# Three operands of Vector's products moved to PSUM, and GpSimd's weight subtractions halved, in a two-block fp32 layer

## Chip, cores and metric

One Trainium2 chip, one core of it, one launch. The time is the device time of that core in microseconds (us). Before the change three runs gave 1184.07, 1188.38 and 1190.91 us, median 1188.38. Engines are called by their function here: TensorE (PE in the rows; PEld is its weight load), Vector (DVE), ScalarE (ACT), GpSimd (POOL) and SyncE (SP), which issues nearly all DMAs.

## What is computed

256 tokens of width 1024 pass two blocks, all in float32; the second also has 16 learned tokens in front, so that it works on 272 columns. Cut to what matters:

```
h    = rms_norm(x)                          # first block
proj = h @ w_in                             # 19 pieces and four gates
y_a..y_d = four mixers of proj              # gating, sparse attention, short convolution, forgetting attention
x1   = x + sum(sigmoid(gates) * (y @ w_branch)) @ w_out
x2   = rms_norm(x1)

h2   = rms_norm([meta; x2])                 # second block, mixer
proj = h2 @ w_in_2                          # f, q, k, v, z, a/b, two gates
q,k,v = silu(depthwise_conv(proj_qkv, 5))   # centred, five taps
A    = strict_lower(beta k k^T * decay)     # per head and chunk of 64 tokens
t    = (I + A)^-1                           # triangular solve
o    = gated delta rule over the chunks, in both directions
y    = gates * ((rms_norm(o) * silu(z)) @ w_delta, fft2(f) @ w_fourier)
h    = h + y @ w_out_2
out  = h + experts(rms_norm(h))             # 64 experts, two for each token
return rms_norm(out)[16:]
```

## The kernel before

**Dense products.** Activations stand feature-major: 128 features on the partitions, tokens in the columns. An fp32 product is made from two exact parts of each factor: a high part that TensorE takes as it is, and the rest. `load()` brings a weight tile in by DMA, ScalarE copies its high part (L293, `whi`), and GpSimd or Vector subtracts that from the whole (L296, `wlo`); a string of letters in `wst["lo"]` says which engine takes which tile, and in the second block's mixer it is GpSimd for most. `dense_fm` (L324) then makes three matmuls for each of eight k: high x high (L331), high x low of the activations (L332) and low of the weights x high (L336), 24 matmuls of 256 or 272 columns for one tile of 128 features, in one PSUM bank `psd`.

**PSUM.** Two kinds of tile: `bank`, one bank, four of them; and `big`, two banks, two of them. Each is given out in turn and is waited for when all are held. `big_c` gives tiles of the same shape in SBUF.

**Stages, in the order of time.** The first block's dense tiles and mixers (0 to about 371 us); the seam, where the first block's result is added up, normed and split into parts (L792 to L855), which `normed` does (L436): Vector builds two diagonal matrices with the rows' factors (L440), TensorE spreads them over the partitions into a bank `psr` (L441), Vector copies that to SBUF (L444, `rcoll`); then for eight feature tiles `x` of `xn` Vector multiplies by `rcoll` (L454), ScalarE copies the high part (L455), and Vector subtracts for the low part (L449). `normed` is called twice, in the first block from the token-major columns (`rcol`) and at the seam. At the seam the factors `rcoll` are also applied to the first two dense tiles of the second block (L847).

The mixer's dense tiles follow (k, q, v with their convolution, then the gates and z), with the delta rule's work woven between. For a convolution tile (`conv`, L996) ScalarE evicts the middle tap from the tile's bank into `acc` (L1004, a part of `ofm`), Vector adds the other four taps from the bank (L1008), ScalarE takes the tanh of the sum into another part of `ofm` (L1011), and Vector multiplies (tanh + 1) by the sum (L1012), into `kr`, `q` or `vr`. There are 24 such tiles, eight each.

For the triangular solve, blocks of 32x32 of A are gathered into `cmp` and transposed in blocks into `am` (L1378); then `substitution` makes 31 steps: step i multiplies the i x i corner of `X` by row i of `am` (L1382, result `xt`), and reduces it to the next column of `X` (L1383). 128 partitions work on 128 blocks at the same time. Its results are merged to blocks of 64 with matmuls, the scans over the chunks follow, then the output, and from some 735 us on the experts, whose weights come in 192 pieces of 1 MB.

**Order.** A scheduler places every instruction on its engine's queue by a simulated time; `weave` and `fill` in the code say how many dense matmuls go between the steps of the delta rule, and `manual_schedule` keeps the written order for some engines in some stretches (Vector's in `normed`). So a change in what an operation reads can move other instructions, too.

Of the kernel before, what the change touches and what calls it, by code (L numbers as in the profile page):

```python
# [33 lines left out]
# no DMA is issued by GpSimd: its descriptors need no room  # L34
# [23 lines left out]
# per-row parameters, broadcast to all partitions  # L58
# [24 lines left out]
def make_constants():  # L83
# [19 lines left out]
    # the transform over the positions, folded twice: cosines for the even and the odd ones, negative sines likewise  # L103
# [74 lines left out]
class Kit:  # L178
# [3 lines left out]
    def ready(self, pool, after, f=AF.Abs_reciprocal_sqrt):  # L182
        """have ACT's table for a function at hand, from the time that a value is there"""
        d = pool.tile([P, 1], F32, name="rs_ready")
        self.nc.scalar.activation(d, after, f, scale=0.0, bias=1.0)

    def rsqrt1(self, y, s, n, b):
        """y = 1/sqrt(s / n + b) from ACT's table, refined once (s: [P, cols], changed; b: [P, 1])"""
        v = self.nc.vector
        bc, bv = b  # L190
        ins = self.nc.scalar.activation(y, s, AF.Abs_reciprocal_sqrt, scale=1.0 / n, bias=bc)
        self.refine(y, s, n, bv)
        return ins
# [10 lines left out]
    def rsqrt(self, pool, y, x, tag):  # L204
        """y = 1/sqrt(x), x > 0"""
# [12 lines left out]
def body(ctx, tc, A, out, dbg=None, stage=9):  # L218
# [11 lines left out]
    # chunks of the experts' weights that come early  # L230
    fix = ctx.enter_context(tc.tile_pool(name="fix", bufs=1))

# [36 lines left out]
    def load(src, width, nsub, view=None):  # L269
        """nsub equal parts of the columns of src, each as (high, low)"""  # L270
# [8 lines left out]
        if wst["pairs"]:  # L279
            # two loads to a tile  # L280
            wst["part"] = 1024 - wst["part"]
# [3 lines left out]
        for j in range(nsub):  # L285
# [10 lines left out]
            eng.tensor_tensor(lo, rs, hi.bitcast(F32), op=ALU.subtract)  # L296
# [3 lines left out]
    def load_tiles(arr, t0, n, k, nsub=None):  # L300
        """n weight tiles of 128 columns, k rows each"""
# [3 lines left out]
    def split_act(pool, name, src, shape, scale=None, tag=None, bufs=None):  # L305
        """f32 tile -> its two exact parts"""
# [10 lines left out]
    def part(x, k, cols):  # L317
        """feature tile k, held in one or several tiles"""
# [5 lines left out]
    def dense_fm(jobs, x, c0, c1, nk):  # L324
        """jobs: (ps, (high, low), offset): ps[128 features, tokens c0:c1], all in one bank"""
# [12 lines left out]
    def dense_tm(pss, subs, x, n, nk, between=None):  # L338
        """pss[t][128 tokens, n columns]; subs cover the rows in order"""
# [17 lines left out]
    def sumsq(junk, src, n):  # L357
        """1 / root of the mean of squares over n columns of a tile, [rows, 1]"""
# [9 lines left out]
    def transpose_scaled(xT, src, rs, c0):  # L368
        """token-major src [rows, 1024], its rows times rs -> columns c0.. of the two parts of the transpose"""
# [11 lines left out]
    def delayed(tile_, src, after):  # L381
        """a load that waits for an earlier one"""
# [11 lines left out]
    # =====================================================================  # L394
    # first block
    # =====================================================================
    b2 = ExitStack()
    with ExitStack() as b1:
# [13 lines left out]
        def turn(pst, src, k, ts):  # L412
            """feature tiles k of token-major src, in PSUM"""
# [5 lines left out]
        def busy(src, n, rhs=None, ps=None):  # L419
            """the PE's clock stays up while it waits"""  # L420
# [6 lines left out]
        def gained(xn, pst, g, ks):  # L427
            """feature tiles ks times their gains"""
# [6 lines left out]
        def normed(xT, c0, xn, r, rcol, then=None, later=None):  # L435
            """columns c0.. of the two parts of the feature-major: the rows of xn times r"""  # L436
# [7 lines left out]
            V.tensor_copy(rcol, psr)  # L444
# [6 lines left out]
            with tc.manual_schedule(engines={V.engine}):  # L451
                for k in range(8):
                    x = xn[k // 4][:, k % 4]
                    V.tensor_tensor(x, x, rcol, op=ALU.mult)  # L454
                    SC.activation(xT[0][:, k, c0:c0 + S], x, AF.Copy)  # L455
                    if k:
                        low(k - 1)
# [17 lines left out]
        # its gains alone, for the token-major columns: those take the rows' factor when they leave PSUM  # L475
# [14 lines left out]
        # ---- token-major columns: c, w_idx, f, d_v, a_v  # L490
# [4 lines left out]
        for j in range(4):  # L495
# [17 lines left out]
            if j == 1:  # L513
# [4 lines left out]
                normed(hT, 0, xn, r1, bp.tile([P, S], F32, name="rcol", tag="th", bufs=3))  # L518
# [13 lines left out]
        # ---- feature-major columns  # L532
# [20 lines left out]
        def gated(o):  # L553
            """o *= silu of the next four tiles"""
# [11 lines left out]
        # ---- the meta tokens, normalised  # L566
# [9 lines left out]
        # ---- y_b: sparse latent attention  # L576
# [19 lines left out]
        def softmax_rows(lm, nk, tag):  # L596
            """lm [P, 4, nk] with its masked entries far below -> p, normalised"""
# [12 lines left out]
        def transposed_p(lm, t):  # L610
            """[P, 4, nk] -> [P (keys), key tile, 4, 128 (queries)]"""
# [50 lines left out]
        # ---- y_d: forgetting attention  # L662
# [11 lines left out]
        # columns k of R[t', h, k] = log f(t') where t' > k  # L674
# [5 lines left out]
        for t in range(2):  # L680
# [3 lines left out]
            # bank kt holds the keys of tile kt, four heads  # L684
# [28 lines left out]
        # ---- y_a: chunked spatial gating  # L713
# [22 lines left out]
        # ---- y_c: short convolution  # L736
# [17 lines left out]
        # ---- gates, branches  # L754
# [20 lines left out]
        # both norms at once, from the sums of squares of x1 and of x1 g  # L775
# [5 lines left out]
        # x1 with its gains, for the first columns of the second block: those take the rows' factor when they leave PSUM  # L781
# [54 lines left out]
        with tc.manual_schedule(engines={PE.engine, V.engine, SC.engine}):  # L836
# [5 lines left out]
            # the second norm sees x1 g over the first one's root  # L842
# [14 lines left out]
    # =====================================================================  # L857
    # second block: mixer
    # =====================================================================
    with b2:  # L860
# [5 lines left out]
        # where the chunks of the experts' weights go, in turn  # L866
# [3 lines left out]
        def buffer(i):  # L870
            """the i-th of the slots; one of 16 KB holds two"""
# [42 lines left out]
        # ---- dense tiles, in the order of their need; the other work is woven in between  # L914
# [53 lines left out]
        # convolution, silu (twice its value)  # L968
# [10 lines left out]
        def row(n, h):  # L979
            return halves(n)[h // 4][:, h % 4]  # L980
# [3 lines left out]
        def of_tile():  # L984
            """blocks of the substitution; two sums of the convolution and their tanh"""
# [4 lines left out]
        def kr_last():  # L990
            """a state of the scans; the fourier branch's input"""
# [4 lines left out]
        def conv(n, off, c0=0):  # L996
            W_ = L - c0

            def use(a, ps):
# [10 lines left out]
                th = of_tile()[:, 1024 + L * (2 + cx["n"]):1024 + L * (2 + cx["n"]) + W_]  # L1010
                SC.activation(th, acc, AF.Tanh, scale=0.5)  # L1011
                V.scalar_tensor_tensor(row(n, a)[:, c0:], th, 1.0, acc, op0=ALU.add, op1=ALU.mult)  # L1012
# [10 lines left out]
        # gate of the delta branch  # L1023
# [9 lines left out]
        # z  # L1033
# [8 lines left out]
        # fourier mixing  # L1042
# [11 lines left out]
        def fold(gs):  # L1054
            """the positions n and L - n at once, then n and L / 2 - n: sums for cosines, differences for sines, of even k and of odd k"""
# [52 lines left out]
        # ---- decays and betas  # L1108
# [6 lines left out]
        # [P, tile, (incl, rest, total), dir, head]  # L1115
        E = ex[:, :96].rearrange("p (t a d h) -> p t a d h", t=2, a=3, d=2)

        def hb(ap, hs=slice(0, 8)):
            """[P, 8] per head -> over 128 columns"""
# [78 lines left out]
        # ---- keys, token-major and feature-major  # L1198
        kn = early.tile([P, 2, 8, P], F32, name="kn")
        knT = keep([P, 8, S], "knT")  # L1200
        def l2(ss, n, tag):
            """per row factor of a doubled vector"""
# [7 lines left out]
        def meta_rows(n):  # L1210
            """the meta tokens of all heads, stacked [(head, token), 128]"""
# [52 lines left out]
        # ---- products of q and k; -beta k k^T with decay (rows: the smaller index)  # L1264
        An = keep([P, 2, 2, 8, P], "An")
        # the earlier steps of the scans, the later ones
# [41 lines left out]
        # ---- the sixteen meta tokens of all heads, stacked  # L1308
# [41 lines left out]
        # ---- (I - An)^-1: blocks of 32 by substitution, then merged  # L1350
        # (in place: forward as it stands, backward transposed)
# [13 lines left out]
        def substitution():  # L1365
# [11 lines left out]
            am = x32(big_c("am"))  # L1377
# [14 lines left out]
        def values():  # L1392
# [17 lines left out]
            # state after the meta tokens  # L1410
# [620 lines left out]
```

## Time and profile before

| | |
|---|---|
| median of three runs | 1188.38 us |
| lowest, highest | 1184.07, 1190.91 us |
| profiled execution, span from first to last instruction | 1187.4 us |
| busy in it: TensorE, Vector, ScalarE, GpSimd | 1064.7, 613.5, 437.6, 386.9 us |
| bytes moved | 307.67 MB, mean 259 GB/s |
| TensorE's granted clock, mean | 0.926 of full |

An engine's busy share is an average over stages with different limits, so the stages are looked at one by one. The profile also follows the chain of work that ended last, back from the last instruction, and gives for each idle stretch of an engine what ended it.

### The profile page before, as it was taken

Reading aid. Unit: us, or ns where it says so; the run is one execution under the profiler, and the core shown is the slowest. Engines: PE = TensorE matmul, PEld = TensorE weight load, DVE = VectorE, ACT = ScalarE, POOL = GpSimd, SP = SyncE. Lnnn points to the kernel's source line nnn. Section 1 sums busy time; section 2 is a strip of 40 time slices with the busy share of each in tenths; the row PEclk is TensorE's granted clock in tenths of the full one; section 3 lists DMA queues with packets and bytes.
Section 4 is the critical chain, followed back from the end, with each engine's and each line's share of the span. In section 5 each row is a group of like instructions: output and inputs, shape, how many; then the busy total and the mean of one; then the engine's idle time right before and its main releaser. Section 6 shows DMA issues by size and latency. Waiting matters only on the chain.

```text
span 1187.4 us, 21273 instructions
## 1 busy us (share of the span) xinstructions
PE 1064.7 (90%) x8800; PEld 855.1 (72%) x8800; DVE 613.5 (52%) x1204; ACT 437.6 (37%) x752; POOL 386.9 (33%) x232
## 2 busy tenths in 40 slices
PE   7899999999998889887999999999978778887794
PEld 7799999999998888887999998455433333333341
DVE  5977647534467998999375885232221111111112
ACT  5555535444447445543533544121111111111112
POOL 4453324456662666866645441000000000000100
PEclk9999999999998989898899999999988887788888
DMA  7444434555554333353227698999999999999993
GB/s 283 166 150 175 143 107 168 188 181 179 202 185 160 122 102 112 108 189 107 73 73 279 261 355 314 403 419 419 421 421 420 421 420 420 420 421 421 420 421 118
DMA packets 58856, 307.67 MB, mean 259 GB/s; under 512 B 5984, under 2 KB 7264, under 8 KB 33280
## 3 DMA queue, kind: packets, MB, share of 16 engines
q1 hardware_dynamic: 56528, 301.59, 65.5%
q10 hardware_dynamic: 2224, 4.65, 1.1%
q8 instruction: 71, 1.16, 0.4%
q14 instruction: 33, 0.27, 0.1%
HBM read 304.12 MB, written 2.10 MB: 258 GB/s over the span
## 4 chain that ended last, share of the span: by engine, by line
PE 59%; DMA 18%; DVE 16%; ACT 3%; issue 1%; POOL 1%; ACTq 0%; SPq 0%; DVEq 0%
DMA wexp<-in_wex_dram 17%; PE psd L331 10%; PE psd L332 10%; PE psd L336 10%; PE psgu L1780 5%; PE psg L1766 4%; PE psy L1819 4%; DVE ofm L1008 3%; DVE xt L1382 2%; PE acc L1833 2%; PE psd L350 1%; PE psd L355 1%; PE psd L349 1%; DVE X L1383 1%; DVE An L1289 1%
## 5 line engine op out<-in xcount | busy, mean ns | idle before, releaser
L296 POOL TENSOR_TENSOR wlo<-wraw,whi 128x1024 fp32r<-128x1024 f32 x115 | 283.7, 2470 | 258.5 <-ACT whi L293 134.6
L331 PE MATMUL psd<-hTh,whi 128*128 128x256 f32 (+2 forms) x1096 | 282.0, 294 | 13.6 <-DVE sz L1037 6.2
L332 PE MATMUL psd<-hTl,whi 128*128 128x256 f32 (+2 forms) x1096 | 280.2, 293 | 4.8 <-DVE hTl L449 4.8
L293 ACT ACTIVATE whi<-wraw 128x1024 fp32r<-128x1024 f32 (+1 forms) x183 | 193.0, 1064 | 172.0 <-PE psd L332 73.5
L331 PEld LDWEIGHTS psd<-hTh,whi 128*128 128x128 f32 x1096 | 215.6, 197 | 16.1 <-issue 10.6
L332 PEld LDWEIGHTS psd<-hTl,whi 128*128 128x128 f32 x1096 | 215.4, 197 | 6.5 <-DVE hTl L449 5.4
L1780 PE MATMUL psgu<-wexp,xg 128*32 128x512 f32 x1024 | 148.8, 671 | 38.0 <-DMA wexp<-in_wex_dram 37.9
L296 DVE TENSOR_TENSOR wlo<-wraw,whi 128x1024 fp32r<-128x1024 f32 (+1 forms) x68 | 121.4, 1791 | 77.0 <-PE psd L336 59.4
L336 PE MATMUL psd<-hTh,wlo 128*128 128x256 f32 (+2 forms) x1096 | 155.8, 290 | 0.0
L336 PEld LDWEIGHTS psd<-hTh,wlo 128*128 128x128 f32 x1096 | 143.0, 195 | 1.6 <-issue 1.4
L1968 POOL TENSOR_SCALAR wexp<-cst,gcol 128x128 f32<-128x128 f32 x8 | 4.7, 599 | 390.5 <-PE psgu L1780 390.5
L1780 PEld LDWEIGHTS psgu<-wexp,xg 128*32 128x32 f32 x1024 | 25.1, 113 | 116.2 <-DMA wexp<-in_wex_dram 85.7
L1766 PEld LDWEIGHTS psg<-pm,x 128*128 128x128 f32 x512 | 76.5, 231 | 16.9 <-issue 12.4
L1819 PE MATMUL psy<-wexp,at 128*32 128x256 f32 x1024 | 78.1, 413 | 9.8 <-DVE at L1809 9.2
L1766 PE MATMUL psg<-pm,x 128*128 128x128 f32 x512 | 84.4, 321 | 0.0
L1828 DVE SCALAR_TENSOR_TENSOR yl<-psy,ww,yh 128x256 fp32r<-128x256 f32 x64 | 31.0, 484 | 102.1 <-ACT yh L1827 97.0
L1786 DVE SCALAR_TENSOR_TENSOR act<-act,psgu 128x256 f32<-128x256 f32 x16 | 6.7, 421 | 136.4 <-ACT act L1785 136.4
L1827 ACT ACTIVATE yh<-psy,ww 128x256 fp32r<-128x256 f32 x64 | 30.3, 474 | 125.8 <-PE psy L1819 120.0
L1785 ACT ACTIVATE act<-psgu 128x256 f32<-128x256 f32 x16 | 6.1, 384 | 140.2 <-PE psgu L1780 140.2
L1819 PEld LDWEIGHTS psy<-wexp,at 128*32 128x32 f32 x1024 | 29.3, 113 | 37.2 <-DVE at L1809 13.5
L1768 DVE TENSOR_SCALAR xg<-psg,gcol 128x128 f32<-128x128 f32 x64 | 22.4, 351 | 62.4 <-ACT xg L1767 61.6
L1767 ACT ACTIVATE xg<-psg,gcol 128x128 f32<-128x128 f32 x64 | 23.5, 368 | 71.7 <-PE psg L1766 71.7
(644 smaller groups left out, 1688.8 us busy)
## 6 DMA issues: line engine op xcount, KB each, us to landing
wexp<-in_wex_dram SPq DMA_DIRECT2D x191, 1024.0 KB, 19.8
wraw<-in_wf_dram SPq DMA_DIRECT2D x39, 1024.0 KB, 4.9
wraw<-in_wf_dram SPq DMA_DIRECT2D x53, 512.0 KB, 4.3
wraw<-in_wbr_dram SPq DMA_DIRECT2D x8, 1024.0 KB, 5.0
wraw<-in_wtok_dram SPq DMA_DIRECT2D x4, 1160.0 KB, 6.7
wraw<-in_wout_dram SPq DMA_DIRECT2D x4, 1024.0 KB, 4.7
wraw<-in_wde_dram SPq DMA_DIRECT2D x8, 512.0 KB, 6.2
wraw<-in_wo_dram SPq DMA_DIRECT2D x8, 512.0 KB, 7.2
```

The lines of the kernel that those rows point to most:

```text
L293: SC.activation(hi, rs, AF.Copy)
L296: eng.tensor_tensor(lo, rs, hi.bitcast(F32), op=ALU.subtract)
L331: PE.matmul(ps, wh[:, ks], part(xh, k, slice(c0, c1)), start=j + k == 0, stop=False, **g)
L332: PE.matmul(ps, wh[:, ks], part(xl, k, slice(c0, c1)), start=False, stop=False, **g)
L336: PE.matmul(ps, wl[:, ks], part(xh, k, slice(c0, c1)), start=False, stop=k == nk - 1, **g)
L1008: V.scalar_tensor_tensor(acc[:, lo:hi], ps[:, lo + d:hi + d], cw(j), acc[:, lo:hi], op0=ALU.mult, op1=ALU.add)
L1382: V.tensor_tensor(tmp[:, :i, :i], X[:, :i, :i], am[:, i:i + 1, :i].to_broadcast([P, i, i]), op=ALU.mult)
L1766: PE.matmul(ps[:, f], hn[:, t, fs], self.pm[:, t].rearrange("p e c -> p (e c)"), start=t == 0, stop=t == 1)
L1780: PE.matmul(gu[32 * q:32 * q + 32, :], self.xg[:, k, 32 * q:32 * q + 32], ws[k][:, 512 * q:512 * q + 512], start=k == 0, stop=k == 7)
L1819: PE.matmul(self.ps[32 * q:32 * q + 32, cs], self.at[:, k, 32 * q:32 * q + 32], self.ws[8 + c][:, o:o + 256], start=k == 0, stop=k == 1)
L1827: SC.activation(yh, self.ps[:, cs], AF.Copy, scale=self.ww)
L1828: V.scalar_tensor_tensor(yl, self.ps[:, cs], self.ww, yh.bitcast(F32), op0=ALU.mult, op1=ALU.subtract)
```

## The change

Four edits. In `normed` Vector's eight products read the factors in PSUM (`psr`) where they lie; the copy to SBUF is ScalarE's, after the third feature tile, and is made only at the seam, where `rcoll` is needed later. In the convolution the tanh is written back into the tile's own bank `ps`, over the raw values, and the last product reads it there. `am` of the substitution lies in a `big` PSUM tile. And where GpSimd subtracts for a low part, it does so in two instructions of half the columns each (512 of 1024); Vector's subtractions stay whole. Comments are gone as well, so line numbers differ by 1 to 3.

```
@@ load
-            eng.tensor_tensor(lo, rs, hi.bitcast(F32), op=ALU.subtract)
+            for h in (slice(0, sw // 2), slice(sw // 2, sw)) if eng is G else (slice(0, sw),):
+                eng.tensor_tensor(lo[:, h], rs[:, h], hi[:, h].bitcast(F32), op=ALU.subtract)
@@ normed
-            V.tensor_copy(rcol, psr)
...
-                    V.tensor_tensor(x, x, rcol, op=ALU.mult)
+                    V.tensor_tensor(x, x, psr, op=ALU.mult)
                     SC.activation(xT[0][:, k, c0:c0 + S], x, AF.Copy)
+                    if k == 2 and rcol is not None:
+                        SC.activation(rcol, psr, AF.Copy)
...
-                normed(hT, 0, xn, r1, bp.tile([P, S], F32, name="rcol", tag="th", bufs=3))
+                normed(hT, 0, xn, r1, None)
@@ conv.use
-                th = of_tile()[:, 1024 + L * (2 + cx["n"]):1024 + L * (2 + cx["n"]) + W_]
-                SC.activation(th, acc, AF.Tanh, scale=0.5)
-                V.scalar_tensor_tensor(row(n, a)[:, c0:], th, 1.0, acc, op0=ALU.add, op1=ALU.mult)
+                SC.activation(ps, acc, AF.Tanh, scale=0.5)
+                V.scalar_tensor_tensor(row(n, a)[:, c0:], ps, 1.0, acc, op0=ALU.add, op1=ALU.mult)
@@ substitution
-            am = x32(big_c("am"))
+            am = x32(big("am"))
```

Vector's queue at the seam before, from the split of the last columns (L795) over the copy of the factors to the feature tiles of `normed`:

```order
L440 TENSOR_SCALAR diag<-cst,r__4227 128x128 x2
L795 TENSOR_TENSOR urows_3881<-xnl,uc_x 128x256 x2
L444 COPY rcoll<-psr 128x256
L454 TENSOR_TENSOR xnh<-xnh,rcoll 128x256 x2
L449 TENSOR_TENSOR hTl_3877<-xnh,hTh_3876 128x256
L454 TENSOR_TENSOR xnh<-xnh,rcoll 128x256
```

And after:

```order
L442 TENSOR_SCALAR diag<-cst,r__4278 128x128 x2
L798 TENSOR_TENSOR urows_3926<-xnl,uc_x 128x256 x2
L455 TENSOR_TENSOR xnh<-xnh,psr 128x256 x2
L450 TENSOR_TENSOR hTl_3922<-xnh,hTh_3921 128x256
L455 TENSOR_TENSOR xnh<-xnh,psr 128x256
```

The copy is gone from Vector's queue, and the products read `psr`; the order of the rest is the same. ScalarE's copy `rcoll<-psr` stands in ScalarE's queue between its third and its fourth feature tile.

Vector's queue over the last steps of the substitution before (`sz` is the product of a z tile, `Xr` the transposed result of the substitution):

```order
L1382 TENSOR_TENSOR xt<-X,am 128x26x26
L1383 TENSOR_REDUCE X<-xt 128x26
L1037 SCALAR_TENSOR_TENSOR sz<-th_5904,psd 128x256
L1037 SCALAR_TENSOR_TENSOR sz<-th_5977,psd 128x256
L1382 TENSOR_TENSOR xt<-X,am 128x27x27
...
L1382 TENSOR_TENSOR xt<-X,am 128x29x29
L1037 SCALAR_TENSOR_TENSOR sz<-th_6028,psd 128x256
L1383 TENSOR_REDUCE X<-xt 128x29
L1382 TENSOR_TENSOR xt<-X,am 128x30x30
L1037 SCALAR_TENSOR_TENSOR sz<-th_6076,psd 128x256
...
L1037 SCALAR_TENSOR_TENSOR sz<-th_6121,psd 128x256
L1387 STREAM_TRANSPOSE Xr<-X 128x1024
```

And after:

```order
L1385 TENSOR_TENSOR xt<-X,am 128x29x29
L1039 SCALAR_TENSOR_TENSOR sz<-th_5987,psd 128x256
L1386 TENSOR_REDUCE X<-xt 128x29
L1385 TENSOR_TENSOR xt<-X,am 128x30x30
L1039 SCALAR_TENSOR_TENSOR sz<-th_6061,psd 128x256
L1386 TENSOR_REDUCE X<-xt 128x30
L1385 TENSOR_TENSOR xt<-X,am 128x31x31
L1386 TENSOR_REDUCE X<-xt 128x31
L1039 SCALAR_TENSOR_TENSOR sz<-th_6113,psd 128x256
L1390 STREAM_TRANSPOSE Xr<-X 128x1024
```

Before, five of the eight z products stood ahead of the transpose `Xr`, the first two behind step 26; after, three do, the first within step 29. On TensorE's queue two dense tiles fewer stand ahead of the first merge.

## Rows read from the trace of the kernel before

**Rows 1.** Table by stages: stretch, length, busy (instructions) per engine, granted clock, DMA.

```profile
core 0: us, PE busy (x) PEld busy (x) DVE busy (x) ACT busy (x) POOL busy (x), PEclk, DMA share, GB/s
60.00:371.00 311.00, 310.51 (x2546) 303.32 (x2545) 180.49 (x222) 155.20 (x225) 144.63 (x71) 0.99 0.49 168
371.00:394.00 23.00, 15.40 (x94) 14.46 (x92) 19.59 (x43) 12.37 (x30) 10.03 (x4) 0.80 0.39 138
394.00:430.00 36.00, 33.35 (x266) 32.28 (x265) 33.57 (x71) 22.84 (x41) 24.89 (x14) 0.97 0.31 105
430.00:561.00 131.00, 114.94 (x806) 108.63 (x807) 123.41 (x237) 58.98 (x88) 87.41 (x48) 0.89 0.36 127
735.00:1140.00 405.00, 339.19 (x2774) 169.11 (x2773) 88.39 (x292) 62.91 (x153) 4.66 (x8) 0.87 1.00 414
```

**Rows 2.** Chain that ended last, 371 to 394 us: start, length, what.

```profile
372.66 4.76 DVE xt L804 x2
...
385.47 2.52 DVE xnh L454
387.99 2.49 DVE hTl L449
```

**Rows 3.** The same chain, 515 to 535 us: shares of the stretch by line.

```profile
by line: DVE xt L1382 83.5%; DVE X L1383 26.7%; issue 2.5%; DVE XRm L1344 1.9%; DVE Zm L1337 1.0%; DVE XCm L1343 1.0%
```

**Rows 4.** Timeline of Vector in the substitution: start, length, line, operation, tiles.

```profile
513.64 2.30 DVE L1382 TENSOR_TENSOR xt<-X,am 128x121 f32<-128x121 f32 x1
...
516.29 0.31 DVE L1382 TENSOR_TENSOR xt<-X,am 128x144 f32<-128x144 f32 x1
516.63 0.30 DVE L1383 TENSOR_REDUCE X<-xt 128x12 f32<-128x144 f32 x1
```

**Rows 5.** Timeline of GpSimd at the seam and in the substitution.

```profile
385.06 5.12 POOL L296 TENSOR_TENSOR wlo<-wraw,whi 128x1024 fp32r<-128x1024 f32 x2 [7.93 <-ACT hTh L455]
...
513.39 2.40 POOL L296 TENSOR_TENSOR wlo<-wraw,whi 128x1024 fp32r<-128x1024 f32 x1
```

**Rows 6.** Operations on the convolution's tile: count, ns minimum/median/maximum, first and last start.

```profile
L1008 DVE SCALAR_TENSOR_TENSOR ofm<-psd,prm,ofm x96: 454/488/501, 394.7 to 509.2; 128x270 f32<-128x270 f32 x32, 128x271 f32<-128x271 f32 x32, 128x256 f32<-128x256 f32 x16, 128x257 f32<-128x257 f32 x16
...
L1012 DVE SCALAR_TENSOR_TENSOR kr<-ofm x8: 423/442/2644, 398.2 to 420.8; 128x272 f32<-128x272 f32 x8
```

**Rows 7.** Vector's groups, 371 to 561 us: count, busy, mean ns, idle before.

```profile
L1382 DVE TENSOR_TENSOR xt<-X,am 128x1 f32<-128x1 f32 (+30 forms) x31 | 34.6, 1116 | 0.8
L1383 DVE TENSOR_REDUCE X<-xt 128x1 f32<-128x1 f32 (+30 forms) x31 | 15.5, 501 | 0.7
L1012 DVE SCALAR_TENSOR_TENSOR q<-ofm 128x258 f32<-128x258 f32 x8 | 8.7, 1083 | 0.9 <-ACT ofm L1011 0.9
...
L1012 DVE SCALAR_TENSOR_TENSOR kr<-ofm 128x272 f32<-128x272 f32 x8 | 8.0, 1025 | 1.0 <-ACT ofm L1011 1.0
L1012 DVE SCALAR_TENSOR_TENSOR vr<-ofm 128x272 f32<-128x272 f32 x8 | 6.3, 793 | 0.6 <-ACT ofm L1011 0.6
...
L1171 DVE TENSOR_TENSOR gu<-mcol 128x1 f32<-128x1 f32 x1 | 1.8, 1843 | 0.0
L1313 DVE TENSOR_SCALAR gUm<-cst,gg 128x128 f32<-128x128 f32 x1 | 1.8, 1753 | 0.0
...
L454 DVE TENSOR_TENSOR xnl<-xnl,rcoll 128x256 f32<-128x256 f32 x4 | 1.6, 412 | 0.0
```

**Rows 8.** Vector's groups of 512 columns over the whole span, by shape.

```profile
L559 DVE SCALAR_TENSOR_TENSOR ob<-th,ob 128x512 f32<-128x512 f32 x2 | 1.4, 693 | 0.1
...
L734 DVE TENSOR_TENSOR a_u<-a_u,pst 128x512 f32<-128x512 f32 x2 | 1.4, 690 | 9.9 <-PE pst L732 9.9
```

**Rows 9.** GpSimd's groups over the whole span, by shape.

```profile
L296 POOL TENSOR_TENSOR wlo<-wraw,whi 128x1024 fp32r<-128x1024 f32 x115 | 283.7, 2470 | 258.5 <-ACT whi L293 134.6 <-PE psd L336 83.2 <-PE psd L355 16.6
...
L727 POOL TENSOR_TENSOR av<-av,rows 128x512 f32<-128x512 f32 x2 | 2.6, 1310 | 1.6 <-DVE lrs L214 1.3 <-DVE av L726 0.4
```

**Rows 10.** TensorE's waits, 371 to 561 us: total us, times, longest.

```profile
PE psd L331 <- DVE sz L1037: 6.2, 1, 6.2
...
PE psd L331 <- DVE ofm L1008: 2.7, 1, 2.7
```

## The prediction

> **What bounds the kernel now.** I read the table of stages first [rows 1]. From 60 to 371 us TensorE is busy 310.51 of 311 us, so nothing that Vector or GpSimd does there can shorten it. From 735 to 1140 us the DMA share is 1.00 at 414 GB/s: the experts' weights stream in. The stream itself cannot be made shorter from this side, but it starts when the stages before it free buffers, so what is gained before 735 us should come off the end about one for one. In between lie stages where Vector is the busy engine: 371 to 394, 19.59 of 23 us; 394 to 430, 33.57 of 36; 430 to 561, 123.41 of 131. From 394 to 561 this is 157.0 of 167 us, while TensorE has 148.3 us and stands idle for 18.7. [...]
>
> Then the chain that ended last. At the seam between the blocks it runs through Vector's products and differences of 128x256, which take 2.4 to 2.5 us each [rows 2]; late in the substitution 83.5% of it is the product L1382 [rows 3].
>
> Last, why these are slow. The product of step 11, 121 elements, took 2.30 us from 513.64; that of step 12, 144 elements, 0.31 us [rows 4]. GpSimd's subtraction of a weight tile ran from 513.39 for 2.40 us [rows 5] and ended at 515.79, 0.15 us ahead of the end of the slow product. GpSimd's pair at 385.06 covers the two slow operations of the seam in the same way. So a Vector operation that starts under a GpSimd subtraction of 1024 columns may wait for its end. But not every one: the convolution's sums L1008, with one operand in PSUM and one in SBUF, took 454 to 501 ns in all of 96 cases, in the same stretches, while the products behind them, L1012, with both operands in SBUF, took up to 2644 ns [rows 6]. What waits is above all Vector with two tensors from SBUF. The change puts one of the two into PSUM in three places, and halves GpSimd's subtractions.
>
> **The change part by part.**
> *Normalisation at the seam.* On the chain stand a pair L804 (4.76 us), one L454 (2.52) and one L449 (2.49) [rows 2]. L454 reads PSUM now and should cost its undisturbed 0.41, that of the four `xnl` ones [rows 7]: -2.1. L449 and L804 keep two SBUF operands; they meet subtractions half as long, so I take half of each: -1.2 and -2.4. The DVE copy goes, a ScalarE copy of the same 256 columns comes, and Vector's fourth product waits for it. I bound that exchange by -0.4 (the copy that goes, if the new one hides under Vector's eight products) and +0.4 (if the whole of the new one is waited for), and take zero, since both are as long. Sum **-5.7**. TensorE is idle for 7.6 us there (23 - 15.40), which is room enough.
>
> *The convolution's last product.* 24 products L1012 take 8.7 + 8.0 + 6.3 = 23.0 us [rows 7]. With one operand in PSUM I take 0.43, between the least (423 ns) and the median (442) of those for `kr` [rows 6]: 24 x 0.43 = 10.3, so **-12.7**. ScalarE's tanh now writes PSUM. No row prices that; between nothing and the whole of an undisturbed product again, 0.4 for each of 24, I take nothing, since ScalarE is busy 81.8 of 167 us and hides it.
>
> *The substitution.* 31 products L1382 take 34.6 us; the reductions L1383 behind them, one SBUF tensor of the same elements, take 15.5 [rows 7], and where neither is caught they are equal: 0.31 and 0.30 at step 12 [rows 4]. **-19.1**. The one transpose that writes `am` into PSUM I count at zero: single, against 62 operations behind it.
>
> *Does reading PSUM cost more?* A product of 512 columns with an operand in PSUM (L734) takes 690 ns, one with both in SBUF (L559) 693 [rows 8]: no. [...]
>
> *Halves.* A subtraction of 1024 columns takes 2.47 at the mean, a GpSimd operation of 512 columns 1.31 [rows 9]: two halves make 2.62, 0.15 more for each of 115 tiles. GpSimd is busy 24.89 of 36 and 87.41 of 131 us in the Vector-bound stages [rows 1], so this hides under Vector's work; if that cover went, the 112.3 / 2.47 = 45 tiles that fit there would cost 7 us. What gains is every Vector operation that is still caught: L1171, one column, took 1.84 us, and L1313 1.75 [rows 7], the latter with a single SBUF tensor, so the rule is a little wider than two operands. Half of some 3 us of such excess is **-1.5**. For the stages before 60 and behind 561 us, with caught operations of the same kind, I put -2 each, about one of the seam's 2.5 us operations each.
>
> *What moves.* Vector's first two products of the z tiles stood behind step 26 of the substitution and stand with steps 29 and 30 now, and two dense tiles fewer stand ahead of the first merge. TensorE waits 6.2 us for such a z product now [rows 10], so that wait may stay, but the substitution ahead of it is shorter by its savings.
>
> **The sum.** In 394 to 561 Vector is relieved of 12.7 + 19.1 + 1.5 = 33.3 us, against TensorE's ceiling of 34.2. Both can't be reached: Vector, at 124 of 134 us, would still be as full as TensorE, and each hand-off between them would have to be free. I take two thirds, 22, because a caught operation is not always the last to arrive. With the seam 5.7 and the two ends 4 the sum is 31.7; I take off 1.7 for the moved z products, about a quarter of their 6.2: **-30**. The profiled execution's span is 1187.4; the median of the runs is 1188.4, 1 us more, so the time is 1188.4 - 30 = 1158.
>
> **The rivals.**
> *All of it comes back* (12 in 100). The ceiling of 34.2 plus seam and ends, 44 us, gives 1144. [...]
>
> *Another engine takes over* (15 in 100). Vector's undisturbed work stays: the 96 sums alone are 96 x 0.488 = 47 us, behind a ScalarE eviction and ahead of a tanh in each tile. If this to and fro sets the pace, a third of the relief shows: 11 + 5.7, so 1171.
>
> *The change doesn't do what it says* (6 in 100): a PSUM operand doesn't free Vector, only the halves help, and each stretch is cut to half: 15 us, 1173. Against it stand the 96 sums without one stretched case [rows 6]. [...]
>
> *No change* (7 in 100): what Vector gains is waited for elsewhere, 1182 to 1194.
>
> *Slower* (8 in 100): PSUM runs short. A convolution tile holds its bank from its first matmul through eviction, sums, tanh and the last product, where it let go after the sums: two operations of 0.43 more, and twice that with queueing; `am` takes one of two big buffers for the whole substitution. When no bank is free TensorE waits. [...] For it speaks that TensorE waits for a convolution sum already; against it, that Vector's queue, which keeps banks waiting, loses 33 us.
>
> **How the numbers follow.** Forecast 1150 to 1168: 52 in 100. The range takes the full return below and the partial gains above with their spread: 1144 to 1178 leaves out the last two cases (15) and a little of the tails. A measurement of this kernel can tell 0.5%, 5.9 us: faster means under 1182.4. Faster 0.52 + 0.12 + 0.15 + 0.06 = 0.85, same 0.07, slower 0.08.
>
> **What would show it.** In the profile after: L1012 and L454 at 0.42 to 0.46 at the maximum, the substitution's products as long as their reductions (if some still take over 1 us, PSUM doesn't free them); GpSimd's low parts at 1.2 to 1.3, twice as many; L804 and L449 at no more than 1.5 instead of 2.5; Vector under 130 us in the stages that were 394 to 561, TensorE idle under 10 us with a granted clock over 0.95. The forecast is wrong if TensorE's waits for a bank (for the convolution's last product) are many and longer than 2.7 us, if ScalarE becomes what TensorE waits for, or if the experts' stage starts no earlier in spite of a shorter mixer.

## The result

The changed kernel takes **1173.16 us** (median of four runs, 1169.84 to 1175.15) against 1189.64 before (the three runs before and a fourth), a ratio of 0.986 with a 95% interval of 0.9835 to 0.9885: 16.5 us faster. The forecast was 1158, with a range of 1144 to 1178. So the sign and the range hold, and the size does not: a little over half of the 30 us came.

On Vector the change did what it says. Vector's groups in the changed kernel, from the seam to the end of the substitution (count, busy us, mean ns, idle before), answer to [rows 7]:

```profile
L1385 DVE TENSOR_TENSOR xt<-X,am 128x1 f32<-128x1 f32 (+30 forms) x31 | 15.6, 502 | 0.8
L1386 DVE TENSOR_REDUCE X<-xt 128x1 f32<-128x1 f32 (+30 forms) x31 | 15.5, 501 | 0.7
...
L1014 DVE SCALAR_TENSOR_TENSOR kr<-psd,ofm 128x272 f32<-128x272 f32 x8 | 3.7, 494 | 0.9 <-ACT psd L1013 0.8
L1014 DVE SCALAR_TENSOR_TENSOR vr<-psd,ofm 128x272 f32<-128x272 f32 x8 | 3.5, 440 | 1.7 <-ACT psd L1013 1.7
...
L1014 DVE SCALAR_TENSOR_TENSOR q<-psd,ofm 128x258 f32<-128x258 f32 x8 | 3.4, 420 | 1.9 <-ACT psd L1013 1.9
...
L1315 DVE TENSOR_SCALAR gUm<-cst,gg 128x128 f32<-128x128 f32 x1 | 1.7, 1725 | 0.0
```

The substitution's products went from 34.6 to 15.6 us, those of the convolution from 23.0 to 10.6. One `kr` product of the 24 still took 0.89 us, where the prediction had 0.46 at the maximum: it stood right behind a small copy (L1169) that took 0.97 us under a GpSimd memset of 0.95. L1315, the L1313 of before, still takes 1.7 us, from 418.11, under a GpSimd product of 1024 columns (`gU`; two of them take 3.75 us from 417.85) that the change does not halve. Vector's busy time over the whole span fell from 613.5 to 545.7 us, by 68; the span fell by 14.0 (1187.4 to 1173.4).

GpSimd's halves, by shape, answer to [rows 9]:

```profile
L298 POOL TENSOR_TENSOR wlo<-wraw,whi 128x512 fp32r<-128x512 f32 x230 | 325.3, 1437 | 233.8 <-ACT whi L293 104.4 <-PE psd L338 67.7 <-issue 26.4
```

Where the time went is read best from one event to the same event in both traces. The last low part of the seam ends 6.5 us earlier than before (387.9 against 394.4), 2.5 of which come from ahead of the pair L807 (the L804 of before) at the seam; the granted clock from 30 to 60 us was 1.00 in this execution and 0.94 in the one before, so these 2.5 may not be the change's. The first step of the substitution starts 7.5 us earlier, the transpose `Xr` behind it 22.1 us earlier, at 538.6. Then the lead shrinks: the transpose of the delta rule's output (`psoT`) starts at 653.6 instead of 664.4, 10.8 us earlier, and the last instruction is 14.0 earlier. The stretch from the seam's end to `psoT`, in the table by stages (stretch, length, busy and instructions of each engine, granted clock, DMA share, GB/s), before:

```profile
394.40:664.40 270.00, 248.53 (x2277) 239.50 (x2277) 220.22 (x410) 127.93 (x194) 168.52 (x103) 0.93 0.39 141
```

and after:

```profile
387.90:653.60 265.70, 249.23 (x2277) 240.50 (x2276) 182.59 (x411) 128.10 (x194) 173.93 (x153) 0.92 0.40 145
```

Vector is relieved of 37.6 us in it, and it is 4.3 us shorter. What sets its length shows if TensorE's idle time and its lost clock, (1 - clock) x stretch, are taken off: 270.0 - 21.5 - 18.9 = 229.6 before, 265.7 - 16.5 - 21.3 = 227.9 after. TensorE's work is some 230 us either way. The idle time fell by 5.0 us, and the clock took some of that back, 2.4 by these rows (their two decimals leave 1.3 open in each). There are new waits; behind the longest of them, the 5.5 us of `psv` below, the granted clock was 0.50 from 492 to 500 us, after 1.00 from 480 to 486. Why the lead shrinks shows when the stretch is divided at `Xr`, before:

```profile
394.40:560.70 166.30, 147.60 (x1069) 140.22 (x1069) 156.28 (x307) 81.42 (x127) 112.00 (x61) 0.91 0.35 121
560.70:664.40 103.70, 100.93 (x1211) 99.29 (x1210) 63.93 (x105) 46.51 (x67) 56.52 (x43) 0.97 0.46 173
```

and after:

```profile
387.90:538.60 150.70, 137.15 (x1016) 130.83 (x1015) 126.79 (x305) 77.91 (x122) 107.47 (x91) 0.92 0.37 132
538.60:653.60 115.00, 112.08 (x1263) 109.67 (x1263) 55.80 (x108) 50.18 (x72) 66.46 (x63) 0.93 0.44 161
```

Up to `Xr` the change is 15.6 us shorter, but with 53 matmuls fewer: they follow behind `Xr`, where there are 52 more and the stretch is 11.3 us longer, at a clock of 0.93 instead of 0.97. Ahead of `Xr` TensorE still stands idle for 13.6 us at a clock of 0.92; the prediction had under 10 us at over 0.95 as the sign of its gain.

TensorE's waits after (line waited at, releaser, us in all, times, longest), from the seam to 735 us:

```profile
PE psv L1405 <- DVE qk L1307: 5.5, 1, 5.5
PE psd L333 <- ACT whi L293: 4.2, 1, 4.2
PE pst L1194 <- DVE q L1014: 2.3, 1, 2.3
```

The 6.2 us for the z product at the end of the substitution are gone, as are the 2.7 for a convolution sum [rows 10]; 5.5 for a big PSUM buffer (the values' transposes wait until Vector has read `psqk`; 1.3 before, for another buffer), 4.2 for a weight's high part (2.4 before) and 2.3 behind a convolution product are new or longer.

### The profile page after: what moved, and what is told of

The parts are those of the page before. It is cut to its first block, busy times and chain, and to the rows that moved or that the text cites. A ratio compares the mean times of both kernels' runs of the same rounds, so it can differ in the third digit from the quotient of the medians.

```text
span 1173.4 us, 21448 instructions
## 1 busy us (share of the span) xinstructions
PE 1056.8 (90%) x8800; PEld 849.1 (72%) x8800; DVE 545.7 (47%) x1202; ACT 437.8 (37%) x753; POOL 426.6 (36%) x347
## 3 DMA queue, kind: packets, MB, share of 16 engines
q8 instruction: 71, 1.16, 0.4%
## 5 line engine op out<-in xcount | busy, mean ns | idle before, releaser
L298 POOL TENSOR_TENSOR wlo<-wraw,whi 128x512 fp32r<-128x512 f32 x230 | 325.3, 1437 | 233.8 <-ACT whi L293 104.4
L333 PE MATMUL psd<-hTh,whi 128*128 128x256 f32 (+2 forms) x1096 | 275.6, 290 | 5.6 <-ACT whi L293 4.6
L334 PE MATMUL psd<-hTl,whi 128*128 128x256 f32 (+2 forms) x1096 | 274.7, 288 | 2.0 <-DVE hTl L450 1.9
L333 PEld LDWEIGHTS psd<-hTh,whi 128*128 128x128 f32 x1096 | 210.4, 192 | 8.0 <-ACT whi L293 5.0
L334 PEld LDWEIGHTS psd<-hTl,whi 128*128 128x128 f32 x1096 | 210.9, 193 | 4.4 <-DVE hTl L450 2.8
L1783 PE MATMUL psgu<-wexp,xg 128*32 128x512 f32 x1024 | 146.0, 659 | 41.6 <-DMA wexp<-in_wex_dram 41.5
L338 PE MATMUL psd<-hTh,wlo 128*128 128x256 f32 (+2 forms) x1096 | 159.7, 292 | 0.0
L298 DVE TENSOR_TENSOR wlo<-wraw,whi 128x1024 fp32r<-128x1024 f32 (+1 forms) x68 | 99.7, 1472 | 81.9 <-PE psd L338 61.9
L1769 PEld LDWEIGHTS psg<-pm,x 128*128 128x128 f32 x512 | 73.6, 223 | 16.6 <-issue 12.0
L1011 DVE SCALAR_TENSOR_TENSOR ofm<-psd,prm,ofm 128x271 f32<-128x271 f32 (+3 forms) x96 | 44.6, 489 | 9.5 <-ACT ofm L1007 8.5
```

The costliest lines, as they stand in the source:

```text
L298: eng.tensor_tensor(lo[:, h], rs[:, h], hi[:, h].bitcast(F32), op=ALU.subtract)
L333: PE.matmul(ps, wh[:, ks], part(xh, k, slice(c0, c1)), start=j + k == 0, stop=False, **g)
L334: PE.matmul(ps, wh[:, ks], part(xl, k, slice(c0, c1)), start=False, stop=False, **g)
L338: PE.matmul(ps, wl[:, ks], part(xh, k, slice(c0, c1)), start=False, stop=k == nk - 1, **g)
L1011: V.scalar_tensor_tensor(acc[:, lo:hi], ps[:, lo + d:hi + d], cw(j), acc[:, lo:hi], op0=ALU.mult, op1=ALU.add)
L1769: PE.matmul(ps[:, f], hn[:, t, fs], self.pm[:, t].rearrange("p e c -> p (e c)"), start=t == 0, stop=t == 1)
```

## The experiments

**Each part alone.** Four kernels, each the kernel before with one hunk of the diff. First the halves:

```
-            eng.tensor_tensor(lo, rs, hi.bitcast(F32), op=ALU.subtract)
+            w_ = sw // 2
+            for h in [slice(q * w_, q * w_ + w_) for q in range(2)] if eng is G else [slice(0, sw)]:
+                eng.tensor_tensor(lo[:, h], rs[:, h], hi[:, h].bitcast(F32), op=ALU.subtract)
```

> The kernel before with GpSimd's halves alone. Theory A (the operations that are caught under a GpSimd subtraction are on the chain, each is caught for half as long): 3 to 8 us faster than before, Vector's busy time falls by 20 to 30 us, L1382 and L1012 stay stretched but end at about 1.3 us. Theory B (two halves cost GpSimd 0.40 us more per tile, 46 us in all, and low parts come late): 0 to 5 us slower, with TensorE's waits for ScalarE's high parts or GpSimd's low parts longer than 2.4 us.

1185.07 us, ratio 0.9955 (0.9935 to 0.9974): 4.6 us faster by the medians, theory A.

The normalisation's products from `psr`, the copy to ScalarE (the hunk `normed`):

> The kernel before with the normalisation's products from PSUM alone. Theory A (the seam's chain gets shorter by the one caught product and the copy, and that carries through): 2 to 4 us faster; the stage from 371 to 394 us is shorter by as much. Theory B (the next caught operation, L449 or L804 with two operands in SBUF, takes the time over): within 1 us of before.

1187.42 us, 0.9976 (0.9959 to 0.9994): 2.2 us, theory A at its lower end. In its trace the way from the pair L804 to the last low part takes 20.4 us, against 21.9 before.

The tanh in the convolution's own bank (the hunk `conv.use`):

> The kernel before with the tanh in the convolution's own bank alone. Theory A (Vector's products are on the way to TensorE's next tile): 4 to 8 us faster. Theory B (the bank is held through the tanh and the last product, and that gives back what Vector gains): within 2 us of before, with the products L1012 at 0.42 to 0.45 us all the same and TensorE's waits in 394 to 510 us no shorter in sum.

1201.11 us, 1.0113 (1.008 to 1.0146): **11 us slower** than before, which neither theory had. The products are relieved all the same: 3.5, 3.3 and 3.3 us for `vr`, `q` and `kr`.

`am` in a big PSUM buffer (the hunk `substitution`):

> The kernel before with the substitution's second operand in PSUM alone. Theory A (the substitution is on the chain, but TensorE's dense work behind it must be done all the same): the substitution ends 15 to 19 us earlier, the program 3 to 8 us. Theory B (the whole of it carries through): 15 us or more faster. Theory C (one of two big buffers is taken, and TensorE's products for the values wait for the other): a wait of 3 us or more before the values' transposes that the kernel before does not have.

1172.90 us, 0.9863 (0.9837 to 0.9888): 16.8 us, as much as all four together. That is theory B, nearly the whole of the 19.1 us of relief carries through; theory A had a third.

**One part left out, and the hold by itself.** If the parts simply added up, the change without its convolution part should have been the best kernel.

> The changed kernel with the convolution's tanh back in SBUF. Theory A (the parts add up, and the convolution's part costs some 11 us because it holds its bank longer): 8 to 12 us faster than the changed kernel, 1161 to 1165 us. Theory B (the convolution's part costs only next to the old order and pays where the substitution is short): as the changed kernel or up to 4 us slower, 1172 to 1177 us.

1182.46 us, 0.9956 (0.9937 to 0.9975). Both theories missed: without the part that costs 11 us alone, the change is 9 us slower than with it.

> The changed kernel with GpSimd's subtractions whole again. Theory A (parts add up, the halves bring 5 us by themselves): 1178 to 1181 us. Theory B (with three operands in PSUM little is left that can be caught, and the halves only cost GpSimd time): 1165 to 1173 us.

1187.63 us, 0.9975 (0.9958 to 0.9992). Without the halves 14 of the 16 us are gone, while the halves alone bring 4.6: further off than theory A, and away from theory B. The order of instructions is another one in this kernel, too (in the traces some 430 of TensorE's 8800 weight loads stand elsewhere than in the change), and was not held, so these 14 us are not the halves' own.

> The changed kernel with the substitution's operand back in SBUF. Theory A (parts add up, the substitution's part alone brings 17 us): 1188 to 1193 us, as slow as the kernel before. Theory B (the substitution is one of several that each bring a share): 1176 to 1182 us.

1192.27 us, 1.0033 (1.0013 to 1.0053), theory A.

So the parts do not add up, and the same hunk is worth +11 or -9 us by what else is there. Two causes were looked at for the convolution's part: the bank that is held longer, or another order of instructions. The first by itself, one small read of the bank behind the last product:

```
                 V.scalar_tensor_tensor(row(n, a)[:, c0:], th, 1.0, acc, op0=ALU.add, op1=ALU.mult)
+                V.tensor_copy(sm.tile([P, 1], F32, name="held", bufs=2), ps[:, 0:1])
```

> The kernel before, all operands where they were, with one more read by Vector of one column of the convolution's bank behind the last product: the bank is held as long as in the change, and no product is relieved. TensorE's order stays that of before. Theory A (the longer hold is what costs): 8 us slower than before or more, with TensorE waiting in 394 to 520 us. Theory B (the hold costs nothing, the convolution's part lost by another order of instructions): 1 to 3 us slower, the price of 24 small reads.

1191.43 us, 1.002 (1.0001 to 1.004): 2.1 us for 24 reads of 0.146 us (3.5 us of Vector in all) and the longer hold together (0.1 to 4.8 by the interval). The order is near that of before, not the same: some 100 of TensorE's 8800 weight loads stand elsewhere in its trace. TensorE does wait for it, but little:

```profile
PE psd L331 <- DVE held L1013: 3.5, 2, 2.6
```

**The same order of instructions.** In the next four kernels an order of another kernel is forced: behind the recording, each of TensorE's and Vector's (in the first three also ScalarE's) instructions is made to follow the one that stands ahead of it in that kernel, without a semaphore (the code is shortened):

```
+        for e_, ix_ in ORDER.items():
+            seq_ = [i for i in nc.cur_bb.bb.instructions if i.engine == eng_]
...
+            for p_, q_ in zip(ix_, ix_[1:]):
+                tc.add_manual_dep(seq_[q_], seq_[p_].name, mybir.DependencyInfo(mybir.DependencyClass.NoSync, mybir.DependencyReason.DATA), reason="order")
```

In the traces of all four, TensorE's weight loads and Vector's instructions stand, by operation, tile and shape, in exactly the order wanted; GpSimd's instructions and the DMAs are left free.

> The kernel before with the convolution's tanh in PSUM alone, as in the run of that part, but with TensorE's, Vector's and ScalarE's instructions held to the order that they have in the kernel before. Theory A (the part lost 11 us because the scheduler put other work between): 1180 to 1189 us, no slower than before. Theory B (the part itself loses, through the bank that is held or ScalarE's writes to PSUM): 1197 us or more, as without the order.

1186.31 us, 0.998 (0.996 to 1.000): the same hunk as in the run that lost 11 us now loses nothing; the 2.4 us that it gains are at the edge of the noise. Theory A. In the traces, without the order held, the waits of TensorE from the seam to `psoT` begin

```profile
PE psk L1241 <- DVE kn L1230: 5.5, 1, 5.5
PE pst L1339 <- DVE Zm L1336: 4.0, 2, 2.6
PE psd L331 <- DVE sz L1036: 4.0, 1, 4.0
PE psqk L1291 <- DVE q L1011: 2.6, 1, 2.6
```

and with it

```profile
PE psd L331 <- DVE sz L1036: 4.6, 1, 4.6
PE pst L1339 <- DVE Zm L1336: 3.2, 1, 3.2
...
PE psk L1241 <- DVE kn L1230: 1.3, 1, 1.3
```

The other way round, the kernel before with every operand where it was, in the order that came with `am` in PSUM:

> The kernel before with its operand of the substitution in SBUF, but in the very order of the kernel that had it in PSUM alone. Theory A (the relieved products are what brought 17 us): 1187 to 1192 us, like before. Theory B (the new order that came with the move to PSUM brought them): 1172 to 1177 us, with L1382 at some 34 us all the same.

1189.78 us, 1.002 (0.9997 to 1.0042), with L1382 at 34.8 us. Theory A: the 17 us are the products' relief, not the order. (The order of before with `am` in PSUM was not tried.)

The substitution's and the convolution's part, both in that order:

> The operand of the substitution and the convolution's tanh both in PSUM, in the order of the kernel with the substitution's operand alone (1172.9 us). Theory A (in one and the same order the convolution's relief costs nothing and brings a little): 1166 to 1173 us. Theory B (the convolution's part loses by itself): 1180 us or more.

1171.69 us, 0.9854 (0.9819 to 0.9888): 1.2 us below `am` alone, no difference that can be told. Theory A as far as it goes.

All four parts, TensorE and Vector in that order:

> The changed kernel with all four parts, TensorE's and Vector's instructions held to the order of the kernel with the substitution's operand alone. Theory A (the parts only fail to add up because each run has another order): 1160 to 1168 us, faster than the change (1173.2) and than that part alone (1172.9). Theory B (the parts stand in each other's way on the chip): 1172 us or more.

**1166.42 us**, 0.9807 (0.9773 to 0.9841), theory A: 22 us faster than before and some 7 faster than the change by the medians. By the ratios it is 6 us (0.9807 against 0.986), with intervals that overlap by a little, on four runs each. Its row for the seam's end to `psoT`, and that of the kernel with `am` alone:

```profile
396.10:647.90 251.80, 239.79 (x2278) 231.01 (x2276) 192.21 (x411) 127.91 (x194) 172.91 (x153) 0.97 0.42 151
```

```profile
394.20:648.30 254.10, 240.83 (x2277) 232.50 (x2277) 206.21 (x410) 127.85 (x194) 167.16 (x103) 0.96 0.41 148
```

251.8 - 12.0 - 7.6 = 232.2 and 254.1 - 13.3 - 10.2 = 230.6: again TensorE's 230 us, with 20 and 23 us of waits and clock on top where the change has 38. Ahead of `Xr` TensorE is idle for 8.6 us at a clock of 0.97 here, with 1066 matmuls:

```profile
396.10:543.60 147.50, 138.88 (x1066) 131.83 (x1065) 127.11 (x307) 81.30 (x127) 113.21 (x95) 0.97 0.40 141
```

The convolution's part alone, in its own order, has 283.2 us:

```profile
392.50:675.70 283.20, 256.24 (x2309) 245.89 (x2308) 217.90 (x412) 127.81 (x194) 171.51 (x104) 0.92 0.37 136
```

that is 233.5 with 27.0 of idle and 22.7 of clock; 32 matmuls more stand in it than before.

## Why the prediction was right, and where not

*The mechanism* was right in each place. A product with one operand in PSUM was not caught: L1014 for `q` is at 420 ns in the mean and 427 at the most, where L1012 was at 1083 in the mean, and the substitution's products take as long as their reductions, 502 and 501 ns. The run with `am` back in SBUF in the same order closes the case for the substitution: the operand alone is worth 17 us. The rival that the change doesn't do what it says falls.

*The step that failed* is the last term of the sum, the 1.7 us for what moves. I had looked at the moved z products and had not asked what else the scheduler moves. In another order the same four parts are 6 to 7 us faster (1166.42), though that difference is near its noise, and in the order of before the convolution's part goes from 1201.11 to 1186.31, 15 us. What the change's order costs is seen in TensorE's new waits and in the 53 matmuls that went behind `Xr`; in the order held, the stretch up to `Xr` is 18.8 us shorter than before (147.5 against 166.3), near the 22 of the forecast. That waits and clock are all of the 6 to 7 us is not shown by itself. They are about half of the 13.5 us that are missing from the forecast; the rest lies in the other terms, below, and how it divides among them is not shown.

*The two thirds* came out in the sum, by luck in its parts. I put both reliefs of Vector under one ceiling, 34.2 us, and took one share of both, which makes 12.7 us for the substitution and 8.5 for the convolution. No run shows that ceiling: it is 18.7 us of TensorE's idle time and 15.5 of its clock, (1 - clock) x stretch [rows 1], with all of both given back. The four parts in the order held leave 8.6 us of idle time and 4.4 of clock up to `Xr`, where the kernel before had 18.7 and 15.0. Measured alone, they are 16.8 of 19.1 (0.9863, and 1.002 without the operand) and 2.4 of 12.7 (0.998, which the noise can make nothing or twice as much). The substitution is a chain of 62 operations on one engine that TensorE waits for behind it [rows 3, 10]. The convolution's tiles are fed by TensorE, which is busy for 33.35 of 36 us at a clock of 0.97 in the stage where the first nine of the 24 products lie [rows 1]: there the ceiling was 2.65 + 1.1 = 3.7 us. For the other 15 this is no full answer. In the two stages behind it TensorE has 2.4 us of idle time at a clock of 0.85, and then 0.8 us at 1.00; before:

```profile
430.00:460.00 30.00, 27.59 (x175) 25.37 (x176) 26.44 (x72) 13.09 (x22) 17.27 (x10) 0.85 0.30 107
460.00:490.00 30.00, 29.21 (x220) 27.07 (x219) 28.90 (x68) 15.87 (x25) 21.61 (x13) 1.00 0.31 106
```

*The 12.7 us* did not all reach Vector's queue, either; part of them went into the next operations. The GpSimd instructions that no longer caught the product caught what came behind it. Vector's timeline with the convolution's part in the order of before (start, length, line, operation, tiles), and GpSimd's beside it:

```profile
427.06 1.78 DVE L1203 TENSOR_SCALAR l2mk<-kss 128x8 f32<-128x8 f32 x1
...
429.15 0.41 DVE L1011 SCALAR_TENSOR_TENSOR q<-psd,ofm 128x258 f32<-128x258 f32 x1
429.48 1.69 DVE L1203 TENSOR_SCALAR l2mk<-kss 128x8 f32<-128x8 f32 x1
431.08 1.94 DVE L209 TENSOR_SCALAR rs_l2k<-l2mk 128x8 int32<-128x8 int32 x1
```

```profile
426.92 1.89 POOL L1128 TENSOR_TENSOR gU<-cst,gg 128x1024 f32<-128x1024 f32 x1
428.77 2.37 POOL L296 TENSOR_TENSOR wlo<-wraw,whi 128x1024 fp32r<-128x1024 f32 x1
431.10 1.89 POOL L1128 TENSOR_TENSOR gU<-cst,gg 128x1024 f32<-128x1024 f32 x1
```

and the same place in the kernel before:

```profile
430.95 0.62 DVE L1204 TENSOR_SCALAR l2mk<-kss 128x8 f32<-128x8 f32 x1
...
431.89 2.28 DVE L1012 SCALAR_TENSOR_TENSOR q<-ofm 128x258 f32<-128x258 f32 x1
434.09 1.86 DVE L1204 TENSOR_SCALAR l2mk<-kss 128x8 f32<-128x8 f32 x1
435.86 0.16 DVE L209 TENSOR_SCALAR rs_l2k<-l2mk 128x8 int32<-128x8 int32 x1
```

The product falls from 2.28 to 0.41, and the first L1203 and L209, eight columns each, go from 0.62 and 0.16 to 1.78 and 1.94. Each of the three slow ones ends within 0.03 us of a GpSimd instruction, two of which are no subtractions but the products `gU`. From the seam to the first of the substitution's blocks (`An`) Vector is busy for 52.43 us in that kernel and for 58.12 before, 5.7 less, where the 14 products in the stretch alone have 9.7 less (6.0 against 15.7); the other 4.0 were passed on to the rest of the same 136 instructions. These small operations read a single SBUF tensor.

*The seam*: -5.7 forecast; the traces show -4.0 (6.5 less the 2.5 that were there before it). The pair L804 goes from 4.84 us to 2.65 and the product L454 from 2.60 to 0.42, as put. The term that failed is L449, -1.2: its eight differences took 5.5 us in all before, one of them caught, and take 5.9 after, with three at 1.16 to 1.18 under four halves that follow each other from 380.15. Vector waits 1.1 us for ScalarE's copy of the factors, behind its third product, where my upper bound was 0.4; but its own copy and other waits are gone, and from `diag` to the fourth product it takes 4.8 us instead of 5.6. Vector's timeline after, and GpSimd's halves:

```profile
370.08 2.65 DVE L807 TENSOR_TENSOR xt<-x,grow 128x256 f32<-128x256 f32 x2
...
380.72 0.42 DVE L455 TENSOR_TENSOR xnh<-xnh,psr 128x256 f32<-128x256 f32 x1 [1.09 <-ACT rcoll L458]
...
381.98 1.18 DVE L450 TENSOR_TENSOR hTl<-xnh,hTh 128x256 fp32r<-128x256 f32 x1
...
383.41 1.16 DVE L450 TENSOR_TENSOR hTl<-xnl,hTh 128x256 fp32r<-128x256 f32 x1
...
384.83 1.17 DVE L450 TENSOR_TENSOR hTl<-xnl,hTh 128x256 fp32r<-128x256 f32 x1
```

```profile
380.15 5.56 POOL L298 TENSOR_TENSOR wlo<-wraw,whi 128x512 fp32r<-128x512 f32 x4 [5.07 <-ACT whi L293]
```

Before, the same of Vector's:

```profile
372.57 4.84 DVE L804 TENSOR_TENSOR xt<-x,grow 128x256 f32<-128x256 f32 x2
...
385.38 2.60 DVE L454 TENSOR_TENSOR xnh<-xnh,rcoll 128x256 f32<-128x256 f32 x1
387.91 2.56 DVE L449 TENSOR_TENSOR hTl<-xnh,hTh 128x256 fp32r<-128x256 f32 x1
```

*The halves*: 0.15 us more for a tile was mis-sized; two of them take 2 x 1.437 = 2.87 instead of 2.47, 0.40 more. The least of them gives 2 x 1.255 = 2.51 against 2.344, 0.17, so the forecast held for undisturbed halves; the rest are halves that take longer, up to 3.069. One of 2.36 us at 114.57 lies beside a Vector subtraction of 1.21 us that starts with it; what stretches the others is not shown. The halves by themselves gain 4.6 us, so their price hides, or is outweighed; their order was not held.

*The rivals.* "Slower", by PSUM that runs short, is not what happened: the bank held longer by itself costs some 2 us, and `am` alone in a big buffer shows no wait for one. The change does show one, the 5.5 us of `psv`, but `am` is not the whole cause: in the changed kernel with `am` back in SBUF TensorE waits 3.1 us at the same place for the same product. Still the part that I had suspected is the one that loses 11 us, for another reason, the order. Nearest in number is "the change doesn't do what it says", 1173, and that is chance, since each product does what the change says. "Another engine takes over" gave 1171; what sets the pace in the change is TensorE's own work of 230 us with the waits that its order leaves, not the to and fro with ScalarE.

## What to carry to other kernels

Take the ceiling for a relief from the stage in which it lies, not from a sum of stages: what the engine that feeds the end has left to gain there, idle and clock, is the most that I would count. When one engine blocks another, relieving the operation that is caught can pass the block on to the next one, as 4.0 of 9.7 us were passed on here; count the engine's whole busy time, not the group's. And, most of all here, where a scheduler sets the order, hold the order fixed before judging an edit: here the same edit cost 11 us in one order and nothing in another.

## What the runs showed of the hardware

Vector's products took the same with an operand in PSUM as undisturbed ones with two in SBUF: 408 to 427 ns for `q` after, 418 at the least before. ScalarE's tanh was faster when it wrote PSUM, operations on the convolution's tile after (count, ns minimum/median/maximum):

```profile
L1013 ACT ACTIVATE psd<-ofm x24: 372/390/403, 391.7 to 504.0; 128x272 f32<-128x272 f32 x16, 128x258 f32<-128x258 f32 x8
```

and before, into SBUF:

```profile
L1011 ACT ACTIVATE ofm<-ofm x24: 405/426/435, 397.7 to 509.8; 128x272 f32<-128x272 f32 x16, 128x258 f32<-128x258 f32 x8
```

36 ns less at the median. And under GpSimd operations of eight columns were stretched as well as products of 272 [rows 6]: L209, 0.16 us in the kernel before, took 1.94 beside a GpSimd product of 1.89.
